# Two transformer blocks in one kernel: the input is loaded first, the first norm's root enters by a diagonal matrix, and the instruction order is fitted anew

## The chip, the core and the metric

The kernel runs on one core of a Trainium2 chip. The core has engines with an instruction stream each: PE (TensorE, matrix products), DVE (VectorE), ACT (ScalarE), POOL (GpSimd) and SP (SyncE, which issues loads). They meet only at semaphores. Products are written to PSUM banks; everything else lies in SBUF. The metric is the time of one execution on the device, in microseconds (us); lower is better. The median of three runs is given, and beside it one more execution that was recorded by the profiler.

## The reference

256 tokens of width 1024 go through two blocks, in float32 (16 meta rows stand ahead of them in the second):

```
h = rms_norm(x, norm_mix_pre)
x = x + rms_norm(hybrid_mixer(h, w_in, ...), norm_mix_post)      # conv branch and forgetting attention
x = x + rms_norm(memory_cross_attention(rms_norm(x), rms_norm(mem), ...), norm_mem_post)
x = x + rms_norm(squared_relu_mlp(rms_norm(x), w_up, w_down), norm_mlp_post)
...
h = h + hybrid_mixer_2(rmsnorm(h, g_mix), ...)                   # SSD scan and short convolution
h = h + peer_ffn(rmsnorm(h, g_ffn), w_q, sub_keys, expert_u, expert_v)
return rmsnorm(h, g_final)
```

`rms_norm(x, g)` is `x / sqrt(mean(x*x) + eps) * g` by row. `peer_ffn` scores each token against 2 x 128 keys in each of 8 heads, takes the best 16 of the 256 sums of the best halves, gathers the 128 expert rows so chosen, and adds gelu(token . u) times the gate times v over them.

## The kernel before

The tokens stand in two row tiles of 128. Dense products are made from pieces: each weight, loaded as float32 in units of 1 MB (128 x 2048), is split on chip into a rounded high part (`scalar.activation` ... `AF.Copy`) and a low part (a subtraction), and three products of high and low parts replace one (`mm3`). A unit has two halves of 128 x 1024: a cast on ACT and a subtraction for each, the latter on DVE in one instruction or on POOL in four of 256 columns (`q.either`).

The program runs in two halves. First the dense one: the first norm, the mixer's products (conv branch, attention), its output projection (`out`, tiles s_281 to s_284, one for each row tile and half of the columns), a seam (`seam1`: the norm of the sum, x plus it, the next norm and its transposes), the memory attention (`mk`, `mq`, `mv`, `recall`, `mo`) whose keys and values of the memory rows are computed where PE has room, a seam, the MLP (`up`, `down`), a seam, the second mixer. Then the experts: for each row tile and head `route` finds the 16 best experts of each token with `max`, `max_index` and `match_replace` on DVE, and casts their numbers to integers (`s_ei`); 16 indirect gathers on POOL each fetch one row of 2048 numbers per token (1 MB, u and v side by side) into a ring of 11 buffers; DVE forms the dot of u with the token (1024 wide), ACT the gelu, PE adds v times a diagonal matrix of the weights. The first route is split in two halves of 8 (`haste`), so that the first gather can be issued early. The second tile's output projection (`again`, tiles s_1051 and s_1052 in the trace's numbering) and norm (`to_n2(1)`) stand in the program behind the first route.

No order is written by hand. Every instruction is recorded in a `Plan` with the engines that may run it, and `Plan.schedule` writes one list per engine before anything runs. The list scheduler takes the instruction with the least start plus a small weight times its place in the program; `block("name")` adds a number from the table `SHIFTS` to the places of a stretch of the program ("name") or of one engine in it ("name.sc" for ACT, ".ve" DVE, ".te" PE, ".sy" SP, ".gp" POOL), and `LATERS` says how much later DVE must be before an instruction that either engine may run goes to POOL. On the chip each engine then works down its list and stands still at the first instruction whose inputs are not there.

The first norm is in the block "start": `normed` takes the squares' sum on ACT, mean and eps on DVE, the power -1/2 on POOL (`nhalf`), and then x times root times gain in one DVE instruction (`scaled`); `transposed` turns the result by 8 transposes for each row tile, four to a PSUM bank, and `split` writes each bank as a high part (ACT, `act<-s`) and a low part (DVE, `act<-s,act`) into `hT`.

All instructions go through one helper line, L544, so that lines do not tell operations apart; the tiles' names do: k8, k4, k2, k1 are pools of buffers by size (shown as k), s and mm PSUM banks, x the two row tiles.

Of the kernel before, what the change touches and what calls it, by code (L numbers as in the profile page):

```python
# [13 lines left out]
BF = mybir.dt.bfloat16  # L14
# [3 lines left out]
ALU = mybir.AluOpType  # L18
AX = mybir.AxisListType

P = 128
D = 1024
# [53 lines left out]
    "mo.gp": 1535, "state3.ve": -1696, "ln.gp": -529, "dt.sy": -251, "dt.sc": 1399, "gate11.sc": -1087,  # L76
# [1823 lines left out]
```

## Time and profile before

| | |
|---|---|
| median of three runs | 1290.63 us (1289.45 to 1291.07) |
| profiled execution | 1292.05 us, its span 1290.3 us |
| PE busy | 1126.7 us (87%) |
| DVE busy | 888.3 us (69%) |
| ACT busy | 536.2 us (42%) |
| POOL busy | 533.1 us (41%) |
| indirect gathers | 256, 268.45 MB |
| other loads and stores on the hardware queue | 108.63 MB |

The span is the time from the first to the last recorded instruction. The shares are means over two halves with different limits, so the rows further down are taken by stretch. "Busy" of PE includes the pipelined length of a product: products follow each other at a smaller distance than one lasts. A row of an engine's timeline gives the start, the time to the end of the last instruction of the group, the instruction, the count, and in brackets the idle time ahead of it with the instruction that ended it.

### The profile page before, as it was taken

How to read it: one execution, taken by the hardware profiler on the slowest of the kernel's cores; microseconds unless marked ns; L12 is line 12 of the kernel's file. 1: busy time of each engine (PE TensorE's matmuls, PEld its weight loads, DVE VectorE, ACT ScalarE, POOL GpSimd, SP SyncE). 2: the span in 40 equal slices, each digit the busy share in tenths (PEclk: the TensorE clock that was granted, in tenths of full speed). 3: DMA queues.
4: the chain of work that ended last, by engine and by line, in shares of the span. 5: the costliest groups of instructions: out<-in, count | busy, mean ns of one | idle time of the engine just before them, and what ended most of it. 6: DMA issues, size and time to landing. Idle time of an engine off the chain costs nothing.

```text
span 1290.3 us, 15247 instructions
## 1 busy us (share of the span) xinstructions
PE 1126.7 (87%) x5047; PEld 772.2 (60%) x5048; DVE 888.3 (69%) x2064; ACT 536.2 (42%) x1084; POOL 533.1 (41%) x529
## 2 busy tenths in 40 slices
PE   5999899999998999999999997877877777777776
PEld 5997687999877899988755563322323222222222
DVE  7887767655657966965899999955555555554555
ACT  6656665544545964542344343223332211212121
POOL 4962453012000666410345535444545545554550
PEclk9999999999998999999999999998999999999999
DMA  7444433554643344438699999999999999999995
GB/s 301 136 160 129 152 143 114 181 198 164 230 182 145 110 152 158 155 137 298 268 423 421 421 420 421 422 422 395 421 422 422 422 422 421 422 422 422 421 421 228
DMA packets 55698, 378.05 MB, mean 293 GB/s; under 512 B 6322, under 2 KB 6962, under 8 KB 11460
## 3 DMA queue, kind: packets, MB, share of 16 engines
q0 software_dynamic: 36864, 268.45, 50.2%
q1 hardware_dynamic: 18756, 108.63, 23.4%
q8 instruction: 40, 0.66, 0.2%
q14 instruction: 38, 0.31, 0.1%
HBM read 376.01 MB, written 1.05 MB: 292 GB/s over the span
## 4 chain that ended last, share of the span: by engine, by line
PE 40%; DMA 36%; DVE 13%; issue 6%; ACT 2%; POOL 2%; POOLq 0%; SPq 0%; DVEq 0%; ACTq 0%
DMA k<-in_uv,s_ei 35%; PE s L544 24%; PE mm L544 17%; DVE k L544 9%; ACT k L544 2%; POOL k L544 1%; DVE s_ix L544 1%; DMA x<-in_x 1%; ACT L544 1%; DVE s_v L544 1%; DVE s_pos L544 1%; DVE act L544 0%; DVE s_best L544 0%; POOL act L544 0%; DVE x L544 0%
## 5 line engine op out<-in xcount | busy, mean ns | idle before, releaser
L544 PE MATMUL s<-k,s_dg 128*128 128x512 f32 x1020 | 475.5, 613 | 121.0 <-ACT s_dg L544 120.8
L544 POOL DMA_INDIRECT k<-in_uv,s_ei x256 | 319.4, 1248 | 317.1 <-DMA k<-in_uv,s_ei 145.6
L544 DVE SCALAR_TENSOR_TENSOR k<-k,k 128x1024 bf16<-128x1024 f32 x256 | 312.9, 1222 | 167.8 <-DMA k<-in_uv,s_ei 166.6
L544 PEld LDWEIGHTS s<-k,s_dg 128*128 128x128 f32 x1020 | 189.7, 194 | 393.4 <-ACT s_dg L544 196.3
L544 PE MATMUL mm<-act,k 128*128 128x256 f32 (+4 forms) x2240 | 316.9, 296 | 2.7 <-DVE k L544 1.9
L544 PEld LDWEIGHTS mm<-act,k 128*128 128x128 f32 x2240 | 294.5, 192 | 16.8 <-issue 5.9
L544 ACT ACTIVATE k<-k 128x1024 fp32r<-128x1024 f32 (+7 forms) x239 | 199.5, 865 | 88.4 <-DVE k L544 37.8
L544 DVE TENSOR_TENSOR k<-k,k 128x1024 fp32r<-128x1024 f32 (+9 forms) x191 | 186.6, 1004 | 65.7 <-ACT k L544 59.3
L544 POOL TENSOR_TENSOR k<-k,k 128x256 fp32r<-128x256 f32 (+2 forms) x198 | 156.4, 826 | 118.5 <-ACT k L544 101.1
L544 PE MATMUL s<-k,k 128*128 128x512 f32 (+6 forms) x832 | 190.1, 371 | 1.6 <-ACT k L544 1.5
L544 ACT ACTIVATE s_act<-s_dots,rx 128x2 f32<-128x2 f32 x129 | 38.1, 295 | 358.1 <-DVE k L544 357.7
L544 PEld LDWEIGHTS s<-k,k 128*128 128x128 f32 (+2 forms) x832 | 143.2, 189 | 34.5 <-issue 6.4
L544 ACT ACTIVATE s_dg<-ident,s_act 128x128 f32<-128x128 f32 x255 | 91.5, 395 | 95.1 <-DVE s_act L544 58.6
L544 PE MATMUL s<-k,act 128*128 128x512 f32 (+1 forms) x432 | 102.5, 379 | 1.6 <-ACT act L544 1.3
L544 PEld LDWEIGHTS s<-k,act 128*128 128x128 f32 x432 | 78.4, 189 | 14.3 <-ACT act L544 1.5
L544 ACT ACTIVATE k<-s 128x512 f32<-128x512 f32 (+8 forms) x99 | 46.5, 484 | 65.8 <-PE s L544 47.7
L544 ACT ACT_TABLE_LOAD x50 | 64.2, 1283 | 6.9 <-DVE s_mx L544 4.1
L544 PE MATMUL s<-ident,k 128*128 128x128 f32 (+2 forms) x220 | 38.4, 301 | 27.5 <-DVE k L544 22.5
L544 POOL TENSOR_TENSOR s_rstd<-s_ms,nhalf 128x1 f32<-128x1 f32 (+1 forms) x15 | 13.5, 902 | 111.6 <-DVE s_ms L544 111.3
L544 POOL TENSOR_TENSOR s_r<-s_ms,nhalf 128x1 f32<-128x1 f32 x10 | 7.8, 777 | 122.9 <-DVE s_ms L544 122.8
L544 ACT ACTIVATE k<-mm 128x256 f32<-128x256 f32 (+2 forms) x70 | 26.3, 376 | 70.9 <-PE mm L544 70.7
L544 PEld LDWEIGHTS s<-ident,k 128*128 128x128 f32 (+2 forms) x220 | 28.2, 152 | 34.3 <-DVE k L544 25.0
(173 smaller groups left out, 740.9 us busy)
## 6 DMA issues: line engine op xcount, KB each, us to landing
k<-in_wts SPq DMA_DIRECT2D x89, 1024.0 KB, 4.8
k<-in_gains SPq DMA_DIRECT2D x9, 512.0 KB, 5.2
k<-in_uv,s_ei POOLq DMA_INDIRECT x256, 19.1
k<-in_wts SPq DMA_DIRECT2D x12, 256.0 KB, 6.3
act<-in_wts SPq DMA_DIRECT2D x4, 512.0 KB, 9.4
x<-in_x SPq DMA_DIRECT2D x2, 512.0 KB, 6.9
k<-in_mem SPq DMA_DIRECT2D x2, 512.0 KB, 6.1
k<-in_sk SPq DMA_DIRECT2D x2, 512.0 KB, 9.1
```

The costliest lines, as they stand in the source:

```text
L544: getattr(getattr(self.nc, e), method)(*a, **kw)
```

## The change

It has two parts. In the block "start", x times the gain is formed first (`xg`), and the root enters as `dg`, a diagonal 128 x 128 matrix (the identity times the root of each row); a product of xg's block with dg scales by the root and turns it in one step, in float32, in place of the transpose.

```diff
-        transposed(hT, normed(xt[i], g_pre), i * P, P)
+
+        xg = k4(D)
+        q.vector.tensor_mul(xg, xt[i], g_pre)
+        r = rstd_of(xt[i], D, q.tile(pool, [P, D], BF, "k2", N2))
+        dg = small(P, "dg", bufs=2)
+        q.vector.tensor_scalar(dg, ident, r, None, op0=ALU.mult)
+        for c in range(0, KD, 4):
+            v = s_bank().rearrange("p (c t) -> p c t", c=4)
+            for j in range(4):
+                q.tensor.matmul(v[:, j], xg[:, (c + j) * P:(c + j + 1) * P], dg, start=True, stop=True)
+            split(hT[0][:, c:c + 4, i * P:i * P + P], hT[1][:, c:c + 4, i * P:i * P + P], v)
```

And nearly all numbers of the two tables are other ones, so every engine's list is in another order, for example:

```diff
 SHIFTS = {
-    "forget": -8106, "start": -6996, "z0": 236, "xs1": -655, "mem": -1368, "gated0": -4534, "gated1": -2004,
+    "forget": -8857, "start": -7630, "z0": 226, "xs1": -632, "mem": -1062, "gated0": -4610, "gated1": -2044,
```

By its lists SP's first loads change from weights, x0, gain, x1, weights, the column table to x0, gain, x1, the column table, weights, weights; then follow, in both, a gain, the memory rows and further weights (before, one more unit of weights stood ahead of these). Tile numbers of the changed kernel are four higher from the first weights on.

ACT's list at the start, before (k8_96 and k8_118 are the first two weight units, k8_256 the memory rows; s_83, s_84, s_89, s_90 the four banks of the first norm):

```order
L544 ACTIVATE k8_97<-k8_96 128x1024
L544 ACTIVATE k8_100<-k8_96 128x1024
L544 ACTIVATE k4_79,s_ss_80<-x0_63 128x1024
L544 ACTIVATE k4_85,s_ss_86<-x1_64 128x1024
L544 ACTIVATE k8_119<-k8_118 128x1024
L544 ACTIVATE thin_105<-colt_66 128x8x8
L544 ACTIVATE k8_122<-k8_118 128x1024
L544 ACTIVATE act_77<-s_83 128x4x128
L544 ACTIVATE act_77<-s_84 128x4x128
L544 ACTIVATE act_77<-s_89 128x4x128
L544 ACTIVATE act_77<-s_90 128x4x128
L544 ACTIVATE k4_257,s_ss_258<-k8_256 128x1024
```

and now (k8_100, k8_122 and k8_260; the banks are s_85, s_86, s_93 and s_94):

```order
L545 ACTIVATE k2_80,s_ss_81<-x0_63 128x1024
L545 ACTIVATE k2_88,s_ss_89<-x1_64 128x1024
L545 ACTIVATE thin_109<-colt_66 128x8x8
L545 ACTIVATE k8_101<-k8_100 128x1024
L545 ACTIVATE k8_104<-k8_100 128x1024
L545 ACTIVATE act_77<-s_85 128x4x128
L545 ACTIVATE k8_123<-k8_122 128x1024
L545 ACTIVATE act_77<-s_86 128x4x128
L545 ACTIVATE k8_126<-k8_122 128x1024
L545 ACTIVATE act_77<-s_93 128x4x128
L545 ACTIVATE k4_261,s_ss_262<-k8_260 128x1024
L545 ACTIVATE act_77<-s_94 128x4x128
```

The squares of x come first now, and the four evacuations of the banks, which stood together, have weight casts and a square of the memory rows between them.

PE's list at the first seam, before (s_283 and s_284 are the last two of the output projection's sums, s_377 and s_378 the sums of the memory values):

```order
L544 MATMUL s_283<-k8_295,act_269 128x512 x2
L544 MATMUL s_283<-k8_295,act_270 128x512
L544 MATMUL s_284<-k8_296,act_269 128x512 x2
L544 MATMUL s_284<-k8_296,act_270 128x512
L544 MATMUL s_284<-k8_296,act_269 128x512 x2
L544 MATMUL s_284<-k8_296,act_270 128x512
L544 MATMUL s_377<-k8_384,act_254 128x512
L544 MATMUL s_377<-k8_384,act_253 128x512 x2
L544 MATMUL s_377<-k8_384,act_254 128x512
L544 MATMUL s_378<-k8_384,act_253 128x512 x2
L544 MATMUL s_378<-k8_384,act_254 128x512
L544 MATMUL s_378<-k8_384,act_253 128x512 x2
```

and now (s_288 is the last of the projection's sums, s_381 and s_382 those of the memory values):

```order
L545 MATMUL s_288<-k8_300,act_274 128x512
L545 MATMUL s_381<-k8_387,act_257 128x512
L545 MATMUL s_381<-k8_387,act_258 128x512
L545 MATMUL s_381<-k8_387,act_257 128x512 x2
L545 MATMUL s_381<-k8_387,act_258 128x512
L545 MATMUL s_382<-k8_387,act_257 128x512
L545 MATMUL s_382<-k8_387,act_258 128x512
L545 MATMUL s_382<-k8_387,act_257 128x512 x2
L545 MATMUL s_382<-k8_387,act_258 128x512
L545 MATMUL s_381<-k8_388,act_257 128x512 x2
L545 MATMUL s_381<-k8_388,act_258 128x512
L545 MATMUL s_381<-k8_388,act_257 128x512 x2
```

Behind the projection's last product stood the last 10 products of the memory values; now 22 of them stand there, and the projection's come 12 products earlier.

DVE's list in the experts, around the indices of the second selection (s_ei_1173, rows 17 to 32), before:

```order
L544 TENSOR_SCALAR s_gt_1178<-s_ge_1175,s_gr_1177 128x16
L544 TENSOR_TENSOR k2_1172<-s_abf_1169,iota16_76 128x256 x2
L544 TENSOR_TENSOR k2_1172<-k2_1172,s_ixf_1163 128x256 x2
L544 TENSOR_TENSOR s_act_1184<-s_act_1184,s_gt_1117 128x2
L544 SCALAR_TENSOR_TENSOR k2_1190,s_dots_1187<-k8_1188,k8_1078 128x1024
L544 TENSOR_REDUCE s_pick_1170<-k2_1172 128x32
L544 SCALAR_TENSOR_TENSOR k2_1191,s_dots_1187<-k8_1189,k8_1078 128x1024
L544 SCALAR_TENSOR_TENSOR s_ef_1171<-s_pick_1170 128x16
L544 SCALAR_TENSOR_TENSOR s_ef_1796<-s_pick_1795 128x16
L544 CAST s_ei_1173<-s_ef_1171 128x16
```

and now (s_ei_1177):

```order
L545 TENSOR_TENSOR k2_1176<-s_abf_1173,iota16_76 128x256 x2
L545 TENSOR_TENSOR k2_1176<-k2_1176,s_ixf_1167 128x256 x2
L545 TENSOR_TENSOR s_act_1204<-s_act_1204,s_gt_1121 128x2
L545 SCALAR_TENSOR_TENSOR k2_1211,s_dots_1207<-k8_1209,k8_1082 128x1024
L545 TENSOR_REDUCE s_pick_1174<-k2_1176 128x32
L545 TENSOR_TENSOR s_act_1212<-s_act_1212,s_gt_1121 128x2
L545 SCALAR_TENSOR_TENSOR s_ef_1543<-s_pick_1542 128x16
L545 SCALAR_TENSOR_TENSOR s_ef_1175<-s_pick_1174 128x16
L545 SCALAR_TENSOR_TENSOR k2_1218,s_dots_1215<-k8_1216,k8_1082 128x1024
L545 CAST s_ei_1177<-s_ef_1175 128x16
L545 CAST s_ei_1545<-s_ef_1543 128x16
```

In both the indices are cast together with those of another selection. The wide products into s_dots are the dots: eight of them stand ahead of the cast of s_ei_1173, thirteen ahead of that of s_ei_1177.

At the memory output four products of another weight unit now follow directly behind the product at which PE waits for a cast, and the first row tile's sums come three products earlier. Between the MLP and the second mixer (the third seam) all lists are as before. In the second mixer's first part (its step sizes and decays) casts, the loads of activation tables and early products are in another order. At the end of the dense half the products and adds of `again` stand ahead of the first scores and of the first `max`.

## Rows read from the trace of the kernel before

**Rows 1.** The page: span, busy share of the DMA engines and GB/s in 40 slices

```profile
span 1290.3 us, 15247 instructions
...
DMA  7444433554643344438699999999999999999995
GB/s 301 136 160 129 152 143 114 181 198 164 230 182 145 110 152 158 155 137 298 268 423 421 421 420 421 422 422 395 421 422 422 422 422 421 422 422 422 421 421 228
```

**Rows 2.** Table by stretch: length, busy PE PEld DVE ACT POOL, clock, DMA, GB/s

```profile
0.00:30.00 30.00, 16.75 (x107) 15.88 (x108) 21.39 (x53) 18.94 (x28) 13.65 (x25) 1.00 0.79 300
150.00:160.00 10.00, 5.01 (x27) 3.79 (x26) 9.97 (x18) 5.95 (x12) 9.87 (x12) 0.91 0.40 122
184.00:200.00 16.00, 11.81 (x54) 8.68 (x52) 11.13 (x18) 7.94 (x16) 8.77 (x10) 0.97 0.18 66
376.00:397.00 21.00, 14.57 (x65) 11.54 (x64) 15.79 (x27) 11.27 (x24) 3.99 (x4) 0.84 0.40 151
405.00:470.00 65.00, 62.61 (x430) 58.40 (x430) 51.14 (x109) 55.29 (x84) 35.32 (x38) 1.00 0.34 120
600.00:630.00 30.00, 27.62 (x158) 24.16 (x157) 20.31 (x64) 10.32 (x20) 1.76 (x3) 0.94 0.74 291
630.00:690.00 60.00, 60.00 (x215) 38.67 (x214) 58.44 (x235) 24.88 (x54) 31.22 (x27) 1.00 0.98 400
```

**Rows 3.** PE in order of time, start: start us, length, instruction, count, idle before

```profile
12.74 3.70 PE L544 MATMUL s<-ident,k 128*128 128x128 f32 x16 [12.74 <-DVE k L544]
...
17.71 3.46 PE L544 MATMUL s<-act,thin 128*64 128x256 f32 x15 [0.51 <-DVE act L544]
...
22.72 4.90 PE L544 MATMUL mm<-act,k 128*128 128x256 f32 x39
27.46 1.03 PE L544 MATMUL s<-ident,k 128*128 128x128 f32 x8
...
618.13 0.39 PE L544 MATMUL s<-k,k 128*128 128x128 f32 x2
```

**Rows 4.** The same of ACT, GpSimd and DVE, start

```profile
5.65 2.00 ACT L544 ACTIVATE k<-k 128x1024 fp32r<-128x1024 f32 x2 [3.64 <-DMA k<-in_wts]
...
10.10 1.06 ACT L544 ACTIVATE k<-x 128x1024 f32<-128x1024 f32 x1 [1.41 <-DMA x<-in_x]
...
14.62 1.60 ACT L544 ACTIVATE act<-s 128x512 fp32r<-128x512 f32 x3
...
9.25 1.37 POOL L544 TENSOR_TENSOR s_rstd<-s_ms,nhalf 128x1 f32<-128x1 f32 x1 [5.30 <-DVE s_ms L544]
...
16.81 0.25 DVE L544 TENSOR_SCALAR trilr<-k 128x128 fp32r<-128x128 f32 x1
16.98 1.27 DVE L544 TENSOR_TENSOR act<-s,act 128x512 fp32r<-128x512 f32 x2
```

**Rows 5.** PE in order of time around the first seam

```profile
142.76 9.46 PE L544 MATMUL s<-k,act 128*128 128x512 f32 x40
...
157.74 0.72 PE L544 MATMUL s<-ident,k 128*128 128x128 f32 x4 [3.87 <-DVE s_ms L544]
```

**Rows 6.** PE in order of time at the memory output

```profile
189.46 5.78 PE L544 MATMUL s<-k,k 128*128 128x512 f32 x24 [1.30 <-ACT k L544]
196.99 0.66 PE L544 MATMUL s<-ident,k 128*128 128x128 f32 x4 [1.76 <-DVE k L544]
```

**Rows 7.** GpSimd's first and 17th gather, DVE around the latter's indices, all gathers' landing

```profile
629.71 1.16 POOL L544 DMA_INDIRECT k<-in_uv,s_ei  x1 [4.37 <-DVE s_gr L544]
...
661.64 1.19 POOL L544 DMA_INDIRECT k<-in_uv,s_ei  x1 [0.78 <-PE s L544]
...
656.51 0.26 DVE L544 CAST s_ei<-s_ef 128x16 int32<-128x16 f32 x2
...
657.25 1.23 DVE L544 SCALAR_TENSOR_TENSOR k<-k,k 128x1024 bf16<-128x1024 f32 x1
...
DMA to landing us min/median/max: 5.6/19.1/20.3
```

More of the change, by code (lines that the diff above doesn't have):

```diff
@@ L52 @@
 SHIFTS = {
[23 rows of a table removed]
-    "mo.gp": 1535, "state3.ve": -1696, "ln.gp": -529, "dt.sy": -251, "dt.sc": 1399, "gate11.sc": -1087,
[84 rows of a table removed]
-LATERS = {
[22 rows of a table removed]
[23 rows of a table added]
+    "mo.gp": 706, "state3.ve": -2210, "ln.gp": -1533, "dt.sy": -1004, "dt.sc": 1667, "gate11.sc": -938,
[85 rows of a table added]
+LATERS = {
[22 rows of a table added]
 SPAN = 3413.3
```

257 rows, old and new, of tables (LATERS, SHIFTS) are left out of this document.

## The prediction

> **What bounds the kernel now.** I read the page first: the span and the slices of DMA [rows 1]. The DMA slices show two programs in one: up to slice 19 the DMA engines are half idle, from slice 20 on they stand at 9 and about 422 GB/s to the last slice. The table by stretch [rows 2] says the same from TensorE's (PE's) side: in the stretches of the first 630 us PE is nearly always busy, apart from a few holes; after 630 the DMA share is 0.98 to 1.0. So the first half (mixers, memory attention, MLP) lasts as long as PE's work plus its holes, and the second half (256 gathers of 1 MB) as long as its bytes, from the moment the first gather can be issued, 629.71 [rows 7]. A microsecond of PE hole removed before that moment is a microsecond of the total; after it only a hole in the DMA stream counts. The holes of the first half that matter, as span less busy time of each stretch [rows 2]: 13.25 us in 0 to 30 (12.74 of it before the first product [rows 3]), 4.99 in 150 to 160, 4.19 in 184 to 200, 6.43 in 376 to 397, 2.39 in 405 to 470, 2.38 in 600 to 630. I then went through the orders at each of these holes.
>
> **The start.** Removed: 16 transposes, 3.70 us [rows 3]. Added: 16 products of xg with a diagonal matrix. A plain fp32 128x128 product has two PE records: 0.39 us for the pair at full rate [rows 3]. The start runs at the slow cadence (15 matmuls of 256 columns in 3.46 us, 0.23 each, against 39 in 4.90, 0.126 each, later [rows 3]; the transposes stand 0.21 apart, as the 3.70 hold the last one's own length of some 0.5), so 16 products cost 32 x 0.21 = 6.8 us, 3.1 more than before. They begin sooner. Loads: a first load of 1 MB had landed by 5.65 and the next 1.5 MB (x0, gain, x1) by 10.10 [rows 4], about 1.48 us for each 0.5 MB. With x0 first it lands at about 5.65 - 1.3 = 4.3, gain 5.7, x1 7.1, the column table 7.8, the first weights about 10.7 (5 us later than now), the second 13.2. xg needs x0 and gain: 5.7 + 1.2 (as a dot product over 128x1024 [rows 7]) = 6.9. Beside it the square, the mean, the root on GpSimd (1.37 [rows 4]) and the small diagonal (0.25, like a 128x128 TENSOR_SCALAR [rows 4]) end at about 9.0. So PE starts at 9.0 instead of 12.74 and has the 16 products done at 15.8 instead of 16.4. That is a gain of only 0.6 there, and the next link is ACT. In the order now the four evacuations of these products (act<-s) follow each other, begun at 14.62 [rows 4]; afterwards they stand between the casts of the first and second weights and the square of the memory rows: the casts take 1.0 each [rows 4] from 10.7 on, so evacuations end at about 13.4, 14.9, 16.5 and 18.4, and the last low part on DVE at about 19.2 (now 18.25 [rows 4]). Behind it stand, by the new order, 52 matmuls of 256 columns and 4 small ones ahead of the first transposes of the memory rows: 52 x 0.126 + 0.5 = 7.0, so these come at 26.2; now they come at 27.46 [rows 3]. **Gain 1.3**, with ends 0 (the last part comes later than 20.5) and 2.0 (PE uses its wait at 16 to 19 fully).
>
> The measured row for loads is the 1.5 MB between 5.65 and 10.10. The Trainium skill (DMA: Bandwidth & Descriptors, Anatomy of one DMA) gives 2.0 us plus bytes over 436 GB/s for a transfer; by that estimate the 2.9 MB ahead of the first cast land at about 9.3 instead of 10.7, and the start would gain 2.7 instead of 1.3. The trace is slower than the page for the same bytes, so the sum goes by the trace.
>
> **The seam behind the first mixer (150 to 160).** PE waits 3.87 us for a mean at 157.74 [rows 5], the end of a chain: last output products, their squares, a root, x plus the scaled sum, its square, the mean. Now the last products of the output projection (s_281 to s_284) are followed by 10 of the memory values' products; the change puts 12 more of these behind them. They cost 9.46/40 = 0.2365 each [rows 5], so the chain starts 12 x 0.2365 = 2.8 us earlier relative to PE's work. Not all arrives: ACT has three weight casts of 1.0 between the squares, and GpSimd the four subtractions of another unit ahead of the second root. I take half: **gain 1.4** (0 to 2.8).
>
> **The memory output (184 to 200).** PE waits 1.30 for a cast weight at 189.46 and 1.76 for the normalised row at 196.99 [rows 6]. Four products of another unit now stand in the first wait (4 x 0.24 = 0.9 of 1.30), and the first row tile's sums end three products earlier (0.7 of 1.76): 0.9 + 0.7 = 1.6, of which I take **1.5** (0 to 3.06, both waits gone).
>
> **Nothing: the seam behind the MLP (376 to 397).** The order of all engines is the same there; 6.43 us stay.
>
> **Unknown: reordered stretches.** In 405 to 470 casts, table loads and the second mixer's early products are in another order; 2.39 us of hole could vanish or come a second time: 0, ends -2.4 and +2.4. From 205 to 340 and from 470 to 590 products of the MLP and of the second mixer are interleaved anew where PE has next to no holes now: that can only lose. The nearest row of a late cast is the 1.30 at 189.46 [rows 6], so 0 to +1.3; I take 0, since the weights are loaded in nearly the same order.
>
> **The end of the first half (600 to 630).** The second tile's last output products and two adds are moved ahead of the first scores. The first selection starts later by 6 products (6 x 0.24 = 1.4), and the second tile's adds are no longer inside its chain on DVE, which shortens that by about as much. I take 0; ends -1 and +1, well inside the 2.38 of hole there [rows 2].
>
> **The start of the gathers.** The order of the selections on DVE changes: the one for rows 17 to 32 comes after 13 dot products instead of 8, together with the one for rows 81 on. Now its cast is at 656.51 and row 17's gather is issued at 661.64 [rows 7]. Five more dots of 1.23 [rows 7] and a little of the other selection are written ahead of it, 7 us more: 663.5 at the earliest. But dot 13 needs row 13, and rows come each 1 MB/422 GB/s = 2.48 us from 629.71 + 5.6 = 635.3 on (5.6 us from issue to landing at the least [rows 7]): 665.1 + 1.2 = 666.3. Where DVE waits for rows between the dots, up to the 5 us that it has nothing to do for ahead of the first, it is 671.5. So the cast comes at 666 to 671.5. Row 17 lands 5.6 later, at 672 to 677; its turn is 635.3 + 16 x 2.48 = 675.0. A gap of 0 to 2.2 in the stream: I take **+0.3**.
>
> **Sum.** -1.3 - 1.4 - 1.5 + 0.3 = -3.9. The profiled run took 1292.05, so 1288.1 for it; it lies 1.4 above the median of the three runs, 1290.63, which gives 1286.7.
>
> **Rivals.** *The start and the seams keep their waits.* For it: behind 15.8 PE has holes in the start, and the slow cadence might last into the dense stream (20 matmuls by 0.23 - 0.126 are 2.1 us, which makes -1.3 into +0.8), and both seams are chains over ACT, DVE and GpSimd that PE's filling does not shorten. Against it: 12 products behind the projection are plain PE time. Then -0.7 to -1.5 is left in the seams: 1290.63 + 0.8 - 1.5 + 0.3 = 1290.2. The Trainium skill (TensorE: Matmul & The Clock Gate, Part 4: PE-mode transpose) says that transposes do not count as activity for the clock; if so, true products from 9.0 on would bring the full rate sooner than the 16 transposes did, which speaks against this rival. No row here tells it: products follow the transposes at once, so a rise of the rate at 21 fits either count.
>
> *Row 17 comes late, and the kernel is slower.* The 13 dots stand ahead of its cast, and each waits for its own row; with them stands the work of two selections instead of one and a part. From a cast at 675.0 - 5.6 = 669.4 on, each us later is a us of idle DMA. If waits between the dots leave half of DVE's time unused and it comes at 679, that is +9.6: 1290.63 - 4.2 + 9.6 = 1296.0. Against: DVE was busy 58.4 of the 60 us behind 630 [rows 2], so it has work to fill its waits with, in the order before at least.
>
> *More comes than I count.* All of the seam's 2.8, 3.06 at the memory output, 2.0 at the start and half of 405 to 470's 2.4: -9 in all, 1281.6.
>
> *The change from the first to the second row tile.* Slice 27 has 395 GB/s instead of 422 [rows 1], a loss of 32.3 x 27/422 = 2.1 us where the gathers go from the first to the second tile. The order there changes too; it can win these 2 us or lose them again. It widens the range.
>
> **Chances.** The sum as worked out (3 to 7 us faster) 0.53; more than that 0.12; the waits stay (within 0.2%, 2.6 us, about what a measurement of this kernel can tell from no change) 0.22; row 17 or a new hole makes it slower 0.13. Faster by over 0.2%: 0.65; within: 0.22; slower: 0.13. The range: from 1281.0 (the third rival with a little of the tile's 2 us) to 1293.0 (the first rival with 2.4 lost in 405 to 470); it leaves out the heavier part of the slower rival.
>
> **What would show it.** In the changed kernel's trace: PE's first product at about 9.0, the first memory transposes at about 26.2; PE's hole in 150 to 160 at about 3.6 instead of 5.0 less the start's shift, in 184 to 200 at about 2.7; 376 to 397 with the same 6.4; the first gather issued at 625.5; no DVE wait for a row around row 17, and a DMA share of 0.98 in the first 60 us behind the first gather. I am wrong if the first product comes at 9 and the memory transposes still at 27.4, if a hole of over 2 us appears where there was none, or if the DMA stream stops around row 17.

## The result, and the profile after

The changed kernel takes 1300.47 us (median of four executions, 1299.39 to 1301.36) against 1290.04 for the kernel before beside it: a ratio of 1.0080, 95% interval 1.0068 to 1.0092. It is slower by 10.4 us where 3.9 less was predicted. The profiled execution took 1299.39 us.

The page of the changed kernel, its span and the GB/s of 40 slices (before: [rows 1]):

```profile
span 1296.8 us, 15269 instructions
...
GB/s 300 131 176 71 189 118 130 163 221 175 192 195 164 98 163 137 143 136 310 243 423 421 421 420 421 421 421 421 421 421 422 421 422 420 422 421 422 420 422 203
```

The second half runs at 421 throughout; the slice of 395 at the change of row tiles is gone. So the loss lies in the first half, and the first gather (GpSimd's timeline) shows it, 7.2 us later than in [rows 7]:

```profile
636.91 1.20 POOL L545 DMA_INDIRECT k<-in_uv,s_ei  x1 [10.00 <-DVE s_gr L545]
...
675.56 0.94 POOL L545 DMA_INDIRECT k<-in_uv,s_ei  x1 [5.93 <-issue]
```

PE's timeline, start, then 75 to 90, first seam, memory output, the seam behind the MLP, and 450:

```profile
9.74 6.27 PE L545 MATMUL s<-s_dg,k 128*128 128x128 f32 x32 [9.74 <-DVE s_dg L545]
...
17.60 1.14 PE L545 MATMUL s<-act,thin 128*64 128x256 f32 x8 [0.60 <-DVE s_ms L545]
...
18.92 0.97 PE L545 MATMUL s<-act,thin 128*64 128x256 f32 x7
...
26.27 1.03 PE L545 MATMUL s<-ident,k 128*128 128x128 f32 x8
...
76.03 3.35 PE L545 MATMUL mm<-act,k 128*128 128x256 f32 x26 [0.47 <-ACT k L545]
82.30 7.46 PE L545 MATMUL mm<-act,k 128*128 128x256 f32 x48 [2.93 <-DVE k L545]
90.01 0.38 PE L545 MATMUL mm<-act,k 128*128 128x256 f32 x1 [0.24 <-ACT k L545]
...
101.09 0.70 PE L545 MATMUL s<-k,inv 128*128 128x256 f32 x2 [0.83 <-DVE k L545]
...
159.02 1.25 PE L545 MATMUL s<-ident,k 128*128 128x128 f32 x8 [1.19 <-DVE k L545]
163.69 1.11 PE L545 MATMUL s<-ident,k 128*128 128x128 f32 x4 [3.42 <-DVE s_ms L545]
165.49 0.58 PE L545 MATMUL mm<-act,k 128*128 128x256 f32 x1 [0.69 <-ACT act L545]
...
201.38 1.23 PE L545 MATMUL s<-ident,k 128*128 128x128 f32 x8 [1.75 <-DVE k L545]
203.42 1.65 PE L545 MATMUL s<-act 128*128 128x512 f32 x3 [0.81 <-DVE act L545]
205.34 1.97 PE L545 MATMUL s<-ident,k 128*128 128x128 f32 x8 [0.27 <-DVE k L545]
...
397.55 1.97 PE L545 MATMUL s<-ident,k 128*128 128x128 f32 x8 [4.87 <-DVE k L545]
...
450.78 4.78 PE L545 MATMUL mm<-act,k 128*128 128x272 f32 x24 [2.95 <-DVE k L545]
```

The hole of 2.93 at 82 has no counterpart before; PE was full there. DVE's timeline and GpSimd's name the reason (a row of GpSimd is from here on a run of subtractions in pieces of 256 columns, each of which starts as the one before ends):

```profile
77.29 4.96 DVE L545 TENSOR_TENSOR k<-k,k 128x1024 fp32r<-128x1024 f32 x1 [3.21 <-POOL k L545]
...
59.65 21.51 POOL L545 TENSOR_TENSOR k<-k,k 128x256 fp32r<-128x256 f32 x31
```

and the same stretch of the kernel before:

```profile
77.18 1.22 DVE L544 TENSOR_TENSOR k<-k,k 128x1024 fp32r<-128x1024 f32 x1 [3.23 <-POOL k L544]
...
59.33 17.11 POOL L544 TENSOR_TENSOR k<-k,k 128x256 fp32r<-128x256 f32 x23
78.11 8.51 POOL L544 TENSOR_TENSOR k<-k,k 128x256 fp32r<-128x256 f32 x12 [1.68 <-ACT k L544]
```

One subtraction on DVE (the low part of a weight that PE needs next) takes 1.22 us before and 4.96 now. GpSimd paused from 76.44 to 78.11 before; now it works without a pause to 81.16, and DVE ends 1.1 behind that. What moved is small: the low part of the first half of a memory key weight, one DVE instruction of 1.30 us at 64.03 before, stands on GpSimd's list now, in four pieces, and fills the pause.

The table by stretch of the changed kernel (columns as in [rows 2]) shows the hole's price:

```profile
79.40:82.30 2.90, 0.00 (x0) 0.00 (x0) 2.90 (x2) 0.38 (x1) 1.77 (x3) 1.00 0.97 331
82.30:86.00 3.70, 3.70 (x20) 3.70 (x21) 3.70 (x10) 0.00 (x0) 0.00 (x0) 0.61 0.73 250
```

PE stands for 2.9 us, and over the next 3.7 the mean granted clock is 0.61, between its levels of 1.2 and 2.4 GHz (0.5 and 1.0): another 3.7 x 0.39 = 1.4 us.

### The profile page after: what moved, and what is told of

It is laid out like the page before. It is cut to its first block, busy times and chain, and to the rows that moved or that the text cites. A ratio compares the mean times of both kernels' runs of the same rounds, so it can differ in the third digit from the quotient of the medians.

```text
span 1296.8 us, 15269 instructions
## 1 busy us (share of the span) xinstructions
PE 1132.0 (87%) x5064; PEld 773.8 (60%) x5064; DVE 891.6 (69%) x2063; ACT 535.5 (41%) x1084; POOL 528.6 (41%) x533
## 5 line engine op out<-in xcount | busy, mean ns | idle before, releaser
L545 POOL DMA_INDIRECT k<-in_uv,s_ei x256 | 316.0, 1234 | 325.6 <-DMA k<-in_uv,s_ei 134.7
L545 ACT ACTIVATE k<-k 128x1024 fp32r<-128x1024 f32 (+8 forms) x239 | 197.8, 866 | 71.8 <-DVE k L545 45.6
L545 DVE TENSOR_TENSOR k<-k,k 128x1024 fp32r<-128x1024 f32 (+8 forms) x190 | 188.0, 1017 | 48.0 <-ACT k L545 42.4
L545 POOL TENSOR_TENSOR k<-k,k 128x256 fp32r<-128x256 f32 (+1 forms) x196 | 153.3, 817 | 125.3 <-ACT k L545 109.7
L545 PE MATMUL s<-k,k 128*128 128x512 f32 (+5 forms) x832 | 187.8, 370 | 0.8 <-ACT k L545 0.4
L545 PEld LDWEIGHTS s<-k,k 128*128 128x128 f32 (+1 forms) x832 | 143.0, 189 | 33.7 <-issue 5.9
L545 DVE TENSOR_TENSOR k<-s,k 128x512 f32<-128x512 f32 (+6 forms) x48 | 26.1, 554 | 31.3 <-ACT k L545 18.8
L545 PE MATMUL s<-ident,k 128*128 128x128 f32 (+2 forms) x204 | 34.1, 292 | 14.2 <-DVE k L545 9.2
L545 DVE SCALAR_TENSOR_TENSOR s<-k,colt,s 128x256 f32<-128x256 f32 x96 | 41.7, 480 | 0.8
```

Of the source, the lines that this page charges most:

```text
L545: getattr(getattr(self.nc, e), method)(*a, **kw)
```

## The experiments

In all of them every engine's list is written out; the diffs say in short which lists, or which instruction of a list, are other ones. Times of places are those of the changed kernel's trace. Ratios are to the kernel before on the same chip, whose medians were 1290.47 (e1 to e4), 1289.74 (e5 to e8), 1289.72 (e9 to e11) and 1289.37 (e12 to e14).

### e1 and e2: the start alone, the start with the seams

```diff
-lists of the kernel before
+lists of the change to 26 us, then those before          (e1)
+the same, and those of the change from 95 to 212 us      (e2)
```

> The changed start (loads, diagonal products, the changed lists up to the first transposes of the memory rows at 26 us), and from there the lists of the kernel before. Theory (the loss is in the later lists: a subtraction on DVE held at 77 to 82 us behind GpSimd's row of subtractions, and further holes): the start alone gains its 1.2 us, 1288.8, and PE has no hole of over 1 us between 30 and 150. Rival (the start does it: weights 5 us later on the queue, so casts come late at 80): 1294 to 1297, with the hole at 82 still there.

> As the run with the changed start only, but between some 95 and 212 us (the first seam, the memory attention) the changed lists; before and behind that the lists of the kernel before. Theory: start 1.2 and seams 2.0 (the distance between the two traces falls from 5.6 at 150 to 3.7 at 200) give 1290.0 - 3.2 = 1286.8. Rival (the seams gain nothing by themselves, the smaller distance only came from the delay ahead of them): 1288.8 as with the start alone.

e1: 1291.57 us, 1.0011 (1.0002 to 1.0019). e2: 1295.11, 1.0046 (1.0031 to 1.0060). Both missed the times that were expected. e1's trace runs 0.5 to 1.8 ahead of the recorded execution before, up to 525, and loses it at 530, where DVE waits for the load of a norm weight of the second mixer (DVE, then SP's list, where the weight is in_ssdn):

```profile
529.33 0.62 DVE L755 SCALAR_TENSOR_TENSOR k<-k,s_rstd,k 128x384 f32<-128x384 f32 x1 [1.20 <-DMA k<-in_ssdn]
...
524.20 0.33 SPq L755 DMA_DIRECT2D k<-in_ssdn  x1
524.62 0.38 SPq L755 DMA_DIRECT2D k<-in_wts  x1
525.09 0.39 SPq L755 DMA_DIRECT2D k<-in_ssdn  x1
```

e2 joins the two orders at a place where they had not done the same work, and new holes of about 1 us stand at its joint, 95 to 98; it shows only that the seams bring nothing like their 2.9. The later splices join at 29, 160, 395 and 584, where the work done differs by two instructions at most, whichever of DVE and GpSimd did it.

### e3 and e4: is it the row of GpSimd?

```diff
 GpSimd
-TENSOR_TENSOR k8_327<-k8_326 x4     (e3: first half's low part, to DVE)
-TENSOR_TENSOR k8_334<-k8_331 x4     (e4: the last four pieces of the row, to DVE)
```

> The changed kernel with one edit: the low part of the first half of the unit k8_326 is formed by DVE in one instruction, as before, and not by GpSimd in four. Theory (GpSimd's unbroken row of subtractions holds the DVE subtraction of 77.3 for 3.7 us; the row is broken and shorter by four pieces): that subtraction takes 1.2 to 1.8 us, PE's hole of 2.93 at 82 falls below 0.5, and with the half clock behind it 4 to 6 us come back: 1295 to 1296.5. Rival (late loads or casts hold PE there): no change, 1300.4.

> The changed kernel with another single edit: the four subtractions that stand behind the held DVE instruction's start in GpSimd's row (second half of the unit k8_331, at 78.4 to 81.2) go to DVE as one. Theory (DVE gets in when GpSimd's row ends, now 78.4): the held instruction ends at about 79.6 instead of 82.25, the other low part at 80.8, PE's hole falls from 2.93 to about 0.6, total 1295.5 to 1298. Rival (DVE is held by a fixed time or by another cause): the instruction again takes 4.96 us and the time stays within 1 us of 1300.4 or rises by the 1.2.

e3: 1294.03, 1.0037 (1.0025 to 1.0049). e4: 1294.54, 1.0037 (1.0024 to 1.0051). Each gives back 0.0043 of the ratio, 5.5 us, by the work of one instruction on another engine, more than was expected. In e3 the subtraction takes 1.23 (at 77.28); in e4 GpSimd's row ends at 78.4 and DVE's subtraction right behind it, after 2.25:

```profile
77.28 2.25 DVE L755 TENSOR_TENSOR k<-k,k 128x1024 fp32r<-128x1024 f32 x1 [3.22 <-POOL k L755]
...
61.76 16.68 POOL L755 TENSOR_TENSOR k<-k,k 128x256 fp32r<-128x256 f32 x24
```

So DVE was held until the row ended. It did not wait for a result of the last four pieces: in e4 their work stands behind it on DVE, at 79.84. By the traces the hold is worth a little less than by the ratios. The product that stands at 90.01 in the changed kernel stands 4.7 earlier in e3:

```profile
85.30 0.38 PE L755 MATMUL mm<-act,k 128*128 128x256 f32 x1 [0.24 <-ACT k L755]
```

In e4 it stands at 85.78, 4.2 earlier, and the 48 products in front of it take 5.96 us at a granted clock of 1.00 instead of 7.46; another 1.5 of what e4 gives back comes at 530, where its norm weight is not late. So the hold is about half of the loss.

### e5 and e11: the same in the kernel before

```diff
 DVE
-TENSOR_TENSOR k8_323<-k8_322        (e5: to GpSimd, as in the change; all else before)
-lists of the kernel before
+lists before to 29 us, those of the change to 160, then those before     (e11)
```

> The kernel before with one assignment of the change alone: the low part of the first half of the weight unit at 64 us, 1.30 us on DVE, goes to GpSimd in four pieces (some 2.1 us) at its place in the list. Theory (a two-input product on DVE that begins beside a long unbroken row of GpSimd's pieces is held until the row ends): GpSimd's row no longer pauses at 76.4, DVE's subtraction at about 76 to 77 takes 4 to 5 us instead of 1.22, PE gets a hole of 2 to 3 us at about 81 that is not there now, and the time is 4 to 6 up, 1294.5 to 1296.5. Rival (the hold needs the rest of the change's order): the subtraction stays below 2 us and the time within 1 us of 1290.5.

> The kernel before with the change's lists from 29 to 160 us alone, the first mixer with the early memory keys, up to the first seam, with nothing mended. If the loss sits in these lists and not in their meeting with the new start: DVE's subtraction at 75 to 77 takes about 5 us, PE has a hole of near 3 us behind it, further holes of 0.5, 0.2 and 0.8 by 100, and the seam keeps its 5: 1296.5 to 1299. If the hold needs the new start's shift, or comes in a part of the executions only as in e5: 1291 to 1294 with single runs at 1297.

e11: 1296.39, 1.0050 (1.0037 to 1.0064), as the first theory had it: with the old start the subtraction takes 4.95 again. e5: 1291.09, 1.0016 (1.0004 to 1.0029), twelve executions from 1288.6 to 1291.9 but for three of 1295.1, 1296.7 and 1296.8. The recorded one, 1288.8, is of the first sort:

```profile
75.53 2.11 DVE L754 TENSOR_TENSOR k<-k,k 128x1024 fp32r<-128x1024 f32 x1 [4.05 <-POOL k L754]
...
59.87 25.98 POOL L754 TENSOR_TENSOR k<-k,k 128x256 fp32r<-128x256 f32 x36
```

GpSimd's row is at least as long as in the changed kernel, yet DVE got in after one further piece. So my theory in its first form (held to the end of a long row) falls: a long row makes a long hold possible, not certain. Lists that are the same word for word up to 395 say so too: the subtraction at 64.6 took 1.22 in e3 and e6 and 2.53 in e13.

```profile
64.64 2.53 DVE L755 TENSOR_TENSOR k<-k,k 128x1024 fp32r<-128x1024 f32 x1
```

### e6, e7, e8 and e14: the change by stretches

```diff
-lists of the kernel before
+e3's lists to 395 us, then those before                            (e6)
+lists before to 395, those of the change to 584, then before       (e7)
+lists before to 160, those of the change to 395, then before       (e8)
+as e8, and those of the change from 584 to the end                 (e14)
```

> The changed kernel with the low part back on DVE (as e3), and from 395 us on, behind the MLP where both lists have done the same work, the lists of the kernel before. If e3's remaining loss of 3.6 us comes from the new order behind 395 (its trace lost 1.7 there): 1290 to 1291. If it lies ahead of 395: 1293 to 1294, with PE at 395 level with the kernel before in the trace and later in the unprofiled runs.

> The kernel before with the change's lists from 395 to 584 us alone, the second mixer; both ends are places where both orders have done the same work. If the new order of the second mixer loses what the changed kernel lost there (2.4 to 3.3 us between 395 and 584): 1292.5 to 1294, first gather 2 to 3 later than 629.7. If the loss there was only the start's shift meeting a load that comes at its own time: within 1 us of 1290.5.

> The kernel before with the change's lists from the first seam (160) to 395 us alone: memory attention, its output, the MLP. By the traces so far PE's holes at the memory output go from 5.8 to about 4.7 and the MLP keeps its time: PE at 395 some 1.0 earlier, time 1289.3. If a lead is lost again at the load of the second mixer's norm weight (as in e1, at 529): 1290 to 1290.5. If the reordered MLP loses 0 to 1.3 as bounded in the prediction: 1290.5 to 1291.5.

> e8 (the change's lists from 160 to 395 us) and also the change's lists from 584 us on: the second tile's products and adds ahead of the first scores, the gathers with rows 17 to 32 behind 13 dots, the change from the first to the second row tile. Prediction's terms for these: 0 (-1 to 1) for the end of the dense half, +0.3 (0 to 2.2) for row 17, the tile's change between -2 and +2. In the traces the changed kernel took 54.3 from 584's place to the first gather against 54.8, and 659.9 from there to the end against 659.3 to 660.6. Expected: within 0.7 of e8, ratio 0.999, time 1287.5 to 1289. If row 17 is late on its own: 1290 or more, with DMA at less than 0.98 in the first 60 us of the gathers.

e6: 1294.05, 1.0031 (1.0018 to 1.0043): what e3 still lost lies mostly ahead of 395, or at the norm weight, which is late in its trace too (4.7 us from issue to landing). e7: 1290.97, 1.0006 (0.9997 to 1.0014), in time the second of its two expectations. e8: 1287.97, 0.9993 (0.9984 to 1.0002). Neither is clear of no change. e14: 1287.56, 0.9982 (0.9973 to 0.9991): faster than the kernel before, and than the changed one by about 1%. It is the version to keep.

e7's trace has the hole of 450 (PE, then the table by stretch), and e8's, with the old lists there, a small one:

```profile
444.98 5.78 PE L754 MATMUL mm<-act,k 128*128 128x272 f32 x24 [2.92 <-DVE k L754]
...
445.00:450.00 5.00, 5.00 (x22) 5.00 (x23) 4.11 (x6) 3.51 (x4) 0.00 (x0) 0.50 0.00 0
```

```profile
439.76 3.29 PE L754 MATMUL mm<-act,k 128*128 128x272 f32 x24 [1.35 <-DVE k L754]
...
439.76:443.05 3.29, 3.29 (x26) 3.26 (x27) 2.54 (x4) 3.23 (x7) 2.78 (x4) 1.00 0.00 0
```

The 24 products behind 2.92 us of standing take 5.78 at a granted clock of 0.50, behind 1.35 they take 3.29 at 1.00. That makes 1.6 and 2.5. e7's recorded execution, 1.4 above its median, runs 2.1 ahead of the recorded one before at 395 and 1.6 behind it at 589: it loses 3.7 there, where the median shows only 0.8. The price of the clock differs between executions. e3 has the hole of 450 too (PE, then the table by stretch), and pays none:

```profile
446.36 3.26 PE L755 MATMUL mm<-act,k 128*128 128x272 f32 x24 [2.95 <-DVE k L755]
...
446.36:449.62 3.26, 3.26 (x25) 3.26 (x26) 3.19 (x6) 3.22 (x4) 0.00 (x0) 1.00 0.00 0
```

In the changed kernel the 24 products take 4.78. That e7's other executions paid less than the recorded one would fit its median, and is not shown.

These traces also tell of the start before, which e5, e7, e8, e11 and e14 run unchanged. In e8:

```profile
12.68 3.64 PE L754 MATMUL s<-ident,k 128*128 128x128 f32 x16 [12.68 <-DVE k L754]
...
17.64 1.93 PE L754 MATMUL s<-act,thin 128*64 128x256 f32 x15 [0.85 <-DVE act L754]
...
25.59 1.04 PE L754 MATMUL s<-ident,k 128*128 128x128 f32 x8
```

The 15 products took 3.46 in the recorded execution that the prediction was made from [rows 3], and 1.92 to 1.97 in all five. The granted clock reads 1.00 in all of them, so only the distance of the products shows it. The record before was an execution with a late start: its memory transposes come at 27.46, those of the five others at 25.5 to 25.75. The change's 26.27 is a gain of 1.2 against the record and a loss of about 0.6 against the others. In these records the new start is the steadier one: in all nine recorded executions with the diagonal products these 15 came at the full rate, behind the transposes in five of seven (not in the record before, nor in e9).

### e9 and e10: the two halves of the start

```diff
-SP: weights, x0, gain, x1, weights, column table
+SP: x0, gain, x1, column table, weights, weights; transposes as before   (e9)
-DVE: x times root times gain; PE: 16 transposes
+DVE: x times gain, diagonal; PE: 16 products; loads as before            (e10)
```

> One half of the change's start: the kernel before with its 16 transposes of the scaled rows, but with the input loaded ahead of the weights and the change's lists up to 26 us; behind it the lists before. To be held against e1, which has the diagonal products in the same lists, and against the start of the kernel before, whose first memory transposes stand at 25.5 to 25.8 in the three traces that ran it at the full clock (e5, e7, e8) and at 27.5 in the one that did not (the kernel before). If the late weight casts between the evacuations on ACT are what holds the new start: the first memory transposes at 26.0 to 26.5 as in e1, time 1290.5 to 1291.5. If the slower products (32 records in 5.2 to 6.7 us against 16 in 3.4) hold it: 25.0 to 25.6, time 1289.5 to 1290.5.

> The other half: the root enters by the 16 products with a diagonal matrix, with the loads and lists of the kernel before (x times gain stands between the two means on DVE, two casts for the heads behind the second diagonal matrix). x is there at 7.5 and 10.1 as before, so the first product comes at about 10.9 instead of 12.7, and the second tile's at about 13.0; 32 records by 0.1 to 0.2 end at 16.3 to 17, as the transposes do now. Expected: first memory transposes at 25.5 to 26.2, time 1289.5 to 1290.7. If the products give the full clock earlier than the transposes do in every run: 25.0, and 0.5 to 1 us less.

e9: 1294.70, 1.0036 (1.0024 to 1.0049), slower than both theories allow. PE waits 3.36 us at 20.73: the last evacuation stands on ACT behind the square of the memory rows, and ACT waits for these rows until 18.58. SP issues them behind their gain, and that at 12.53, in e1 at 9.01 (PE and SP of e9, then SP of e1):

```profile
20.73 1.97 PE L754 MATMUL s<-act,thin 128*64 128x256 f32 x8 [3.36 <-DVE s_ms L754]
...
12.53 0.33 SPq L754 DMA_DIRECT2D k<-in_gains  x1
```

```profile
9.01 0.33 SPq L755 DMA_DIRECT2D k<-in_gains  x1
```

This gain needs one of the four k4 buffers. With the diagonal products it takes that of the first gain, which is free once x1 is multiplied by it, at 8.99, before any root is known; with the old scaling it gets that of the first scaled row, which PE's first eight transposes have read at 12.50. Behind the wait the 15 products come at half the rate, 1.97 and 1.64 us where e1 has 1.15 and 0.96, another 1.5. So e9 does not tell the load order's own price; it shows that the load order needs the early product x times gain. e10: 1292.72, 1.0018 (1.0008 to 1.0027): the first product at 10.88 as expected, but 6.02 for the 32 records, and the memory transposes at 27.18, 1.4 to 1.7 later than in the old start and later than expected. Its trace loses another 2.6 at 530, where the norm weight lands 5.1 behind its issue, so its ratio is not that of the start alone. Neither half was seen to gain; together, with the norm weight mended, they come out even (e12).

### e12 and e13: the late norm weight

```diff
 SP
 DMA k2_922<-in_ssdn
-DMA k8_1013<-in_wts
 DMA k2_846<-in_ssdn
+DMA k8_1013<-in_wts          (e12: in e1's lists; e13: in e6's)
```

> e1 (the change's start, the lists before behind it) with one move on SP: of the three loads at 524 us the weight unit of 1 MB goes behind the second norm weight instead of between the two. In the traces that lost 1.3 to 2.6 us at 530 (changed kernel, e1, e2, e3, e6, e10) the first norm weight landed 4.6 to 5.1 us after its issue, the weights' issue taking 0.38 and the second norm weight following 0.9 behind the first; in the others (before, e5, e7, e8, e9, e11) it landed after 3.0 to 3.7, and those 0.9 were 1.25 to 2.0. If the large load close behind the small one delays it: the first now lands within 3.7, DVE waits for no load at 529, the holes of 0.61 and 0.24 at 530 go, and the time is 1 to 2 below e1's ratio of 1.0011: 1289 to 1290. If the small load is late for another reason: 4.6 to 5.1 again, DVE waits 0.9 to 1.3, time as e1.

> The changed kernel with all that the runs found mended but the start, the holes at 76 to 101 and the first seam: the low part back on DVE, the lists before from 395 us on, the same move on SP (e6 and e12 in one). e6 is 1.0031. If the late norm weight is worth 1 to 2 us here: 1291.5 to 1293. If the account of the parts (start +0.6, 76 to 101 +1.2, seam +0.3, memory output and MLP -0.9 in us) is complete: 1290.5 to 1292. If neither: 1293.5 to 1295.

e12: 1289.71, 0.9999 (0.9989 to 1.0008). e13: 1291.19, 1.0017 (1.0006 to 1.0029). The move is worth 0.0012 of the ratio to e1 and 0.0014 to e6, 1.5 to 1.8 us, neither by itself clear of its uncertainty (1.7 and 2.2). The landing times of the two norm weights, from issue, of e1 and then of e12:

```profile
DMA to landing us min/median/max: 5.0/6.1/7.1
```

```profile
DMA to landing us min/median/max: 3.1/4.2/5.3
```

In e12 the first lands 3.1 behind its issue, and no DVE instruction waits for it. So the small load was late because of the place of the 1 MB load. That this load begins 0.4 us behind it is not enough: it does so in all the traces but those of e12 and e13. In the six where the first small load was late, the 1 MB load took 0.38 us to issue and the second small one came 0.9 behind the first; in the eight others 0.6 to 1.5 and 1.1 to 2.0 (in the kernel before 0.75 and 1.26). Why some of these programs issue them closer together was not found.

**The account**, by ratios: the hold at 82, 5.5 us (e3, e4); the norm weight, 1.5 (e12); 395 to 584, 0.8 (e7); the start itself, 0 (e12); 160 to 395, -0.9 (e8); from 584 on, -1.4 (e14 to e8); and 29 to 160 besides the hold, between 0.9 (e11's 6.4 less 5.5) and 3.2 (e13 less e12 and e8). Of that the trace places 1.2 in the holes of 0.47, 0.24 and 0.83 between 76 and 101, where the old lists have one of 0.32. The sum is 6.4 to 8.7 of 10.4. A term that is one ratio is uncertain by about 1.2, one that is a difference of two by 1.6 to 2.2, so 395 to 584, 160 to 395 and the stretch from 584 on are not clear of zero, and the rest is not proof of a further cause. The traces place nearly all of it. e7 runs the lists before up to 395, from a start that was not late; against it the seam behind the MLP comes 7.0 later in the changed kernel (397.55), 0.5 of that from the start. PE in e7, then in the kernel before:

```profile
390.53 1.97 PE L754 MATMUL s<-ident,k 128*128 128x128 f32 x8 [4.86 <-DVE k L754]
```

```profile
392.63 1.97 PE L544 MATMUL s<-ident,k 128*128 128x128 f32 x8 [4.86 <-DVE k L544]
```

From there to the first gather it takes 239.4 us against 237.1 before, which makes 9.3. Holds that come in some executions only (as perhaps in e5's three slow ones, which were not recorded, and as the 2.53 in e13) would fit the rest, and were seen in no record at that size besides 82.

## Why the prediction was wrong

**What bounds the kernel** was right: what PE lost ahead of the first gather came out at the end, and the gathers kept their rate.

**The step that failed first is the choice of stretches.** The sum went through the stretches in which the record before has holes, and the prediction named 205 to 340 and 470 to 590 as reordered where "that can only lose", and 405 to 470 as unknown. 29 to 160 was in neither list but for its seam, though the change reorders it: PE was full there, so it had nothing to win, and was given no price and no bound. It cost 6.4 us (e11). The price of "the nearest row of a late cast", 1.30, would not have covered it either. In the trace and the lists the material was there: GpSimd's row of 23 pieces beside DVE's two-input subtractions, and the four pieces that the new lists add to it. One of the prediction's own signs of being wrong, a hole of over 2 us where there was none, is what came.

**The start.** The parts were right: first product 9.74 (9.0 predicted), 32 records 6.27 (6.8), first cast of a weight at 10.86 (10.7), memory transposes 26.27 (26.2). The estimate of 9.3 for that cast's data by the Trainium skill (DMA: Bandwidth & Descriptors, Anatomy of one DMA), a fit made there for a transfer on GpSimd's path, does not hold here, where SP puts five loads into one queue. The rate of the trace did. The term of -1.3 was wrong all the same, since the 27.46 that it was subtracted from belongs to a late-starting execution. The text took "the slow cadence" for a property of the start, and the record's distance from the median (1.4 in the text, 2.0 by the second set of runs) for noise to take off at the end; it was this cadence, so the gain was counted against a loss that none of the five other recorded executions of that start has. Against them the start is even (e12). My rival's worry, the slow cadence lasting into the dense stream, did not happen: the 15 products take 1.14 and 0.97.

**The first seam**, -1.4: came out +0.3. The holes are 1.19, 3.42 and 0.69, 5.30 together, where before [rows 5] the stretch 150 to 160 had 4.99 [rows 2]. Twelve more products in front shortened the wait for the mean by 0.45; the half that I took was a guess, and a second wait (for the sum on DVE) grew by 0.64. The rival "the seams keep their waits" was right here.

**The memory output**, -1.5: right. The wait of 1.30 [rows 6] is gone, the others are 1.75, 0.81 and 0.27: 2.8 instead of the 4.19 in [rows 2]. e8 measures -0.9 (-2.1 to 0.3) for all of 160 to 395. **The seam behind the MLP** keeps its 4.87, and with three small ones 6.4, as said.

**405 to 470 and 470 to 590.** The value 0 was wrong and the bounds of 2.4 and 1.3 a little small: the hole at 450 cost 1.6 more than before and its clock 1.5 in the changed kernel's trace, and the norm weight 1.5 to 1.8. The latter is no late cast but a load; its queue had not been looked at.

**The end of the dense half and row 17**: right. Row 17's gather is issued 38.6 behind the first one (31.9 before) and, like before, lands 47 behind it; the stream has no gap there. The rival of a late row 17 gave the slower end its time, 1296.0, by a mechanism that did not occur. The slice of 395 GB/s vanished, but no gain by it is shown: from the first gather to the last landing it is 650.0 against 650.8 before, and 649.5 in e8, which has the old order there.

## What to carry to other kernels

Where a change writes all lists anew, go through every stretch it touches, the full ones above all: a stretch without holes has only a loss to give, and needs a bound like any other. Ask of each list what moved between DVE and GpSimd and how long GpSimd's unbroken row becomes beside DVE's two-input instructions. And before an execution's start or seam is taken as the time to beat, hold its record against the median: where it lies above, find the place first.

## What the runs showed of the hardware

**A DVE instruction can be passed by more than once.** I took all 16 recorded executions, up to 620 us, and every two-input TENSOR_TENSOR on DVE of over 1.15 us that began inside a piece of GpSimd's row with another piece directly behind, 168 in all. Where fewer than 14 pieces had gone before in the row, DVE got in at the next boundary each time, 120 of 120. Where 14 or more had, it was passed by in 14 of 48, by one or two pieces mostly, by five in the changed kernel and in e11. The Trainium skill (SBUF — State Buffer, SBUF: two separate sides, and Who interferes with whom) says that a DVE instruction with two SBUF inputs contends with a GpSimd instruction that reads SBUF, and that the first to issue keeps the pair of ports for the whole instruction while the other fully blocks. The 120 agree: the wait is for the one piece under way, and the longest of them took 1.76 us, 0.5 more than the 1.22 of an undisturbed one. The 14 don't: pieces that began after DVE's instruction went ahead of it. In the 34 others with as many pieces in front it got in at the next boundary, so no trace shows a hold without a long row, and a long row is not enough. Whether the count of pieces or the time since the row began (over 10 us in all 14) matters, and what else decides, no run here tells.

**What a hole costs in clock differs between executions.** Behind holes of 2.9 us the granted clock was 0.61 over 3.7 us in the changed kernel at 82 (1.4 us lost), 0.50 over 5 us in e7 at 445 (2.5 lost), and 1.00 in e3 at 446. Behind 1.35 in e8 it was 1.00.

**A small load can land later when large and small ones follow closely**: the norm weight of 384 numbers for each partition took 4.6 to 5.1 us in the six traces where a 1 MB load took 0.38 us to issue right behind it and the next small load came 0.9 behind, 3.0 to 3.7 in the others and 3.1 and 3.5 with the 1 MB load behind both (e12, e13).
